# Four of six conditioning quads move from the recurrence to the next two norms' borders, where products use both PSUM bank rings

## The chip, the cores and the metric

One core of one Trainium2 chip runs the kernel. The metric is the device time of one execution in microseconds (us). The engines run their own streams of instructions and wait for one another by semaphores: TensorE (PE; its weight loads are listed as PEld), VectorE (DVE), ScalarE (ACT), GpSimd (POOL), and SyncE (SP), which here issues the DMAs.

## The reference, cut to what matters

One step of a trunk of two layers on 1024 prompt rows and 8 single decode rows. Layer 0 mixes by a gated linear recurrence with 8 heads (HGRN2), layer 1 by sliding-window attention over K and V that are projected once, after layer 0. Every sub-layer is scaled, shifted and gated by vectors of the condition c:

```
def rms_norm(x, g):
    x32 = x.astype(jnp.float32)
    y = x32 * lax.rsqrt(jnp.mean(x32 * x32, axis=-1, keepdims=True) + EPS)
    return y * g.astype(jnp.float32)

def modulate(x, g, shift, scale):
    return rms_norm(x, g) * (1.0 + scale[:, None, :]) + shift[:, None, :]

def ada_params(c, w, b):
    return (jax.nn.silu(c) @ w + b).astype(jnp.float32)

def swiglu(x, w_in, w_out):
    gate, up = jnp.split(x @ w_in, 2, axis=-1)
    return (jax.nn.silu(gate) * up) @ w_out

for l in range(DEPTH):                       # DEPTH = 2, D_MODEL = 1024
    sh1, sc1, g1, sh2, sc2, g2 = jnp.split(ada_params(c, w_ada[l], b_ada[l]), 6, axis=-1)
    xn = modulate(h, norm_w[l, 0], sh1, sc1)
    mix = hgrn2_mixer(xn, ...) if l < N_A_LAYERS else swa(xn @ w_q_b[j], k_sh, v_sh, ...) @ w_o_b[j]
    h = h + g1[:, None, :] * mix
    xn = modulate(h, norm_w[l, 1], sh2, sc2)
    h = h + g2[:, None, :] * swiglu(xn, w_ffn_in[l], w_ffn_out[l])
    if l == N_A_LAYERS - 1:
        sh_kv, sc_kv = jnp.split(ada_params(c, w_ada_kv, b_ada_kv), 2, axis=-1)
        k_sh, v_sh = jnp.split(modulate(h, kv_norm_w, sh_kv, sc_kv) @ w_kv, 2, axis=-1)
```

The conditioning is thus c (9 rows, the prompt's and the 8 samples') times 14 x 1024 columns of weights: 2 x 6 x 1024 of w_ada and 2 x 1024 of w_ada_kv.

## The kernel before, in words

All products keep about fp32 accuracy: a weight and a moving operand are each split into a high and a low part, and mm3 (L275 to L278) issues three matmuls for each tile of 128 rows. The 1032 columns (1024 prompt rows and 8 decode rows) go in three chunks of 344 (grouping G3) or in four of 258 (G4). A product's PSUM bank comes from one of two rings of four banks: mmp, tag "mm", and axp, tag "ax"; a product that takes its bank from mmp has four banks to run ahead in. The result is added to the residual stream h by VectorE (residual, L665, and L669 for the decode columns), which frees the bank.

**Conditioning.** The 14 x 1024 columns are seven "quads" of 2048 columns. A quad is eight steps (ada_step, L464), one for each 128 rows of the weight: two tiles of 128 x 1024 (512 KB each) are loaded (ada_unit, L269), and four fp32 matmuls with the 32-column stationary tile cT, one for each column group of TensorE, add 512 columns each into one bank. ada_end copies the bank, turns it by four transposes (L478) and adds the bias; mod_scale(m) makes the scale of norm m from it. Quad 0 is done at the start. Quads 1 to 6 are done in the recurrence: hgrn_proj(hh), heads 1 to 6, does two steps behind each of its four projections. Quad 6 is that of w_ada_kv. Norm 1 is the norm before the FFN of layer 0, 2 that before K/V, 3 that before q, 4 that before the FFN of layer 1. cT lies in a single buffer with the tag "early"; the tile "late" (the attention's biases) takes the same buffer later and is filled by 16 small DMAs in biases (L1075, L1076), which ffn(0) calls in its middle.

**Recurrence.** run interleaves two generators, hgrn_proj of a head (three chunks of four projections) and hgrn_core of the head before it, by a ratio.

**Border 1.** wo_first and wo_second multiply the two halves of the attention output with w_o. wo_second goes over four chunks of 258 and eight row tiles n, each one wo_product of 12 matmuls, then N.square for the norm's sums; finishing a chunk's norm and applying it is put on a list (later), and step() takes one piece of it at a time. Then ffn(0) begins with the gate and up products (proj). Beside them factors(x) makes sums and differences of x's four quarters for a product in seven parts in place of eight; diff and part (L1175 to L1183, L1193, L1194) are wide VectorE instructions, and L1234 adds a bank of a seven-part product. The same code makes border 3 in layer 1, from the sliding-window attention's output.

**Border 2.** The last pass of ffn(0) is again wo_product, three chunks of 344, with the norm before K/V (ToKV) beside it; then h is stored to hsc (L1404), four K/V products a chunk follow, and the norm before q is applied to X beside them. Weights are loaded by split_unit (L188) through three buffers named raw, cast on ScalarE (L175) and subtracted on GpSimd (L178).

The engines' streams are laid out when the program is built: each engine works its own list in order. SP's list has all the loads and stores of this kernel, so a DMA that waits holds those behind it.

## Time and profile before

| | us |
|---|---|
| median of 3 runs | 2582.14 (2582.01 to 2587.13) |
| the profiled execution | 2581.89 |
| its span | 2580.1 |

The profile's page gives the busy time of each engine and the chain of work that ended last. The costliest groups of instructions on TensorE and VectorE, by line, engine and operation, then the operands (out<-in), the shapes, the count, the busy time with the mean in ns of one, and the idle time ahead of them with what ended most of it:

```profile
L276 PE MATMUL mm<-c,wu 128*128 128x344 f32 (+1 forms) x2544 | 819.9, 323 | 21.4 <-DVE tdec L669 7.5
L276 PE MATMUL mm<-xq,wu 128*128 128x258 f32 x1448 | 412.1, 285 | 11.2 <-DVE c L1234 10.2
L665 DVE SCALAR_TENSOR_TENSOR c<-mm,ada,c 128x344 f32<-128x344 f32 (+3 forms) x400 | 220.6, 556 | 266.2 <-PE mm L278 265.2
```

A matmul of 344 columns starts every 0.16 us while its record is about 0.32 us long, because neighbours overlap; so the cost of a piece of TensorE work is read from start to start. The conditioning's loads are 96 tiles of w_ada and 16 of w_ada_kv:

```profile
c<-in_w_ada_dram SPq DMA_DIRECT2D x96, 512.0 KB
c<-in_w_ada_kv_dram SPq DMA_DIRECT2D x16, 512.0 KB
```

### The profile page before, as it was taken

The page shows a single profiled execution, that of the slowest core. Times are in us where ns is not written, and L with a number is a line of the kernel's source. Part 1 is how long each engine was busy: PE and PEld are TensorE (multiplying, and loading weights), DVE is VectorE, ACT ScalarE, POOL GpSimd, SP SyncE. Part 2 cuts the span into 40 slices and gives each one's busy share as a digit, 9 for nine tenths or more (in the row PEclk, how much of TensorE's full clock was granted, in tenths as well). Part 3 has the DMA queues.
Part 4 walks back from the last instruction along what each step waited for, and adds up shares of the span by engine and source line. Part 5 has one row for each costly group of instructions (what it writes and reads, how often), then busy time and mean ns, then how long its engine had stood idle before and what let it go on. Part 6 is the DMA issues. An engine that isn't in the chain of part 4 may idle for free.

```text
span 2580.1 us, 51430 instructions
## 1 busy us (share of the span) xinstructions
PE 2473.3 (96%) x21003; PEld 2337.4 (91%) x21003; DVE 1446.8 (56%) x3313; ACT 852.3 (33%) x1962; POOL 812.0 (31%) x604
## 2 busy tenths in 40 slices
PE   7999999999989999999999999999899999999998
PEld 5988888898989999999999897878899999999998
DVE  5343444446697554655433844576975555555336
ACT  4323222223343332333211445555433333332212
POOL 1211121212324443544432221203244444444321
PEclk9999999999999999999999999999999999999999
DMA  9464555514222224225421321432212222254201
GB/s 323 157 218 154 175 183 182 182 60 141 67 99 83 75 76 125 83 83 191 156 76 47 99 54 58 139 110 72 99 59 88 85 75 75 75 205 144 87 26 66
DMA packets 264670, 293.37 MB, mean 114 GB/s; under 512 B 28969, under 2 KB 223418, under 8 KB 264402
## 3 DMA queue, kind: packets, MB, share of 16 engines
q1 hardware_dynamic: 264032, 289.86, 34.1%
q8 instruction: 165, 2.70, 0.4%
q14 instruction: 71, 0.58, 0.1%
q10 hardware_dynamic: 402, 0.22, 0.0%
HBM read 231.27 MB, written 63.99 MB: 114 GB/s over the span
## 4 chain that ended last, share of the span: by engine, by line
PE 79%; DVE 12%; issue 4%; DMA 2%; ACT 1%; POOL 1%; SPq 1%; DVEq 0%; POOLq 0%; ACTq 0%
PE mm L276 18%; PE mm L278 18%; PE mm L277 18%; PE ax L276 5%; PE ax L277 5%; PE ax L278 5%; DVE w L646 2%; PE ax L1649 1%; PE ax L1578 1%; DMA c<-in_w_ada_dram 1%; PE ax L864 1%; PE ax L1635 1%; DVE xq L651 1%; DVE c L1182 1%; DVE c L1181 1%
## 5 line engine op out<-in xcount | busy, mean ns | idle before, releaser
L178 POOL TENSOR_TENSOR wu<-raw,wu 128x512 fp32r<-128x512 f32 x460 | 633.5, 1385 | 1397.4 <-ACT wu L175 1242.3
L276 PE MATMUL mm<-c,wu 128*128 128x344 f32 (+1 forms) x2544 | 819.9, 323 | 21.4 <-DVE tdec L669 7.5
L277 PE MATMUL mm<-c,wu 128*128 128x344 f32 (+1 forms) x2544 | 812.0, 319 | 8.0 <-DVE c L1313 6.5
L278 PE MATMUL mm<-c,wu 128*128 128x344 f32 (+1 forms) x2544 | 812.2, 319 | 0.3 <-issue 0.3
L276 PEld LDWEIGHTS mm<-c,wu 128*128 128x128 f32 x2544 | 482.3, 190 | 42.7 <-issue 22.3
L277 PEld LDWEIGHTS mm<-c,wu 128*128 128x128 f32 x2544 | 483.3, 190 | 12.8 <-DVE c L1313 7.6
L278 PEld LDWEIGHTS mm<-c,wu 128*128 128x128 f32 x2544 | 482.9, 190 | 4.9 <-issue 4.1
L175 ACT CAST wu<-raw 128x512 fp32r<-128x512 f32 x460 | 282.7, 620 | 593.7 <-PE mm L278 279.2
L276 PE MATMUL mm<-xq,wu 128*128 128x258 f32 x1448 | 412.1, 285 | 11.2 <-DVE c L1234 10.2
L278 PE MATMUL mm<-xq,wu 128*128 128x258 f32 x1448 | 411.4, 284 | 0.8 <-POOL wu L178 0.8
L277 PE MATMUL mm<-xq,wu 128*128 128x258 f32 x1448 | 411.5, 284 | 0.0
L665 DVE SCALAR_TENSOR_TENSOR c<-mm,ada,c 128x344 f32<-128x344 f32 (+3 forms) x400 | 220.6, 556 | 266.2 <-PE mm L278 265.2
L276 PE MATMUL ax<-xq,wu 128*128 128x258 f32 x1064 | 301.3, 283 | 0.0
L277 PE MATMUL ax<-xq,wu 128*128 128x258 f32 x1064 | 301.2, 283 | 0.0
L278 PE MATMUL ax<-xq,wu 128*128 128x258 f32 x1064 | 300.6, 283 | 0.0
L276 PEld LDWEIGHTS mm<-xq,wu 128*128 128x128 f32 x1448 | 275.1, 190 | 12.9 <-DVE c L1234 11.1
L278 PEld LDWEIGHTS mm<-xq,wu 128*128 128x128 f32 x1448 | 275.6, 190 | 1.2 <-POOL wu L178 1.1
L277 PEld LDWEIGHTS mm<-xq,wu 128*128 128x128 f32 x1448 | 275.9, 191 | 0.1
L277 PEld LDWEIGHTS ax<-xq,wu 128*128 128x128 f32 x1064 | 202.0, 190 | 0.0
L276 PEld LDWEIGHTS ax<-xq,wu 128*128 128x128 f32 x1064 | 201.6, 190 | 0.0
L278 PEld LDWEIGHTS ax<-xq,wu 128*128 128x128 f32 x1064 | 201.6, 189 | 0.0
L767 DVE TENSOR_TENSOR c<-c,mm 128x344 f32<-128x344 f32 x42 | 21.4, 513 | 126.6 <-ACT c L765 126.6
(301 smaller groups left out, 2831.2 us busy)
## 6 DMA issues: line engine op xcount, KB each, us to landing
c<-in_w_ada_dram SPq DMA_DIRECT2D x96, 512.0 KB
raw<-in_w_ffn_in_dram SPq DMA_DIRECT2D x152, 256.0 KB
ff<-c SPq DMA_DIRECT2D x44, 516.0 KB
c<-ff SPq DMA_DIRECT2D x44, 516.0 KB
raw<-in_w_ffn_out_dram SPq DMA_DIRECT2D x44, 512.0 KB
raw<-in_w_in_a_dram SPq DMA_DIRECT2D x32, 512.0 KB
out_dram<-c SPq DMA_DIRECT2D x16, 512.0 KB
c<-in_w_ada_kv_dram SPq DMA_DIRECT2D x16, 512.0 KB
```

The source lines that it names most:

```text
L175: i = act.copy(u[:, 0, :], src)
L178: eng.tensor_tensor(u[:, 1, :], src, u[:, 0, :], op=ALU.subtract)
L276: pe.matmul(ps, wh, xh, start=first, stop=False)
L277: pe.matmul(ps, wh, xl, start=False, stop=False)
L278: pe.matmul(ps, wl, xh, start=False, stop=last)
L646: dve.scalar_tensor_tensor(t, h[k][:, s], modA[:, m, k, 0:1], self.R[:, s], op0=ALU.mult, op1=ALU.mult)
L651: dve.scalar_tensor_tensor(xl, t, shift, xh, op0=ALU.add, op1=ALU.subtract)
L665: dve.scalar_tensor_tensor(hc, ps[:, : g.pl[c]], ada[:, gate + n, 0:1], hc, op0=ALU.mult, op1=ALU.add)
L864: pe.matmul(ps[32 * j : 32 * j + 32, c * 32 : (c + 1) * 32], KS[:, t0 : t0 + 32], QP[:, t0 : t0 + 32], start=True, stop=True, tile_positio ...
L1181: dve.tensor_tensor(t, flat(p[0]), flat(q[0]), op=ALU.subtract)
L1182: dve.tensor_tensor(e, flat(p[1]), flat(q[1]), op=ALU.subtract)
L1578: pe.matmul(psv[hf][:, gi, s0:256], q[2 * gp + gi][r, tb * P : (tb + 1) * P], kT[a][r, (tb - 1) * P + s0 : (tb + 1) * P], start=True, stop ...
```

## The change

The diff does six things. (1) anyp gives banks from the two rings in turn; wo_second and the last pass of ffn use it, in both layers. (2) The order in which conditioning tiles are loaded becomes quads 1, 2, 6, 3, 4, 5. (3) In the recurrence only heads 1 to 4 do conditioning, one step behind each projection: quad 1 in heads 1 and 2, quad 2 in heads 3 and 4. (4) A generator, conditioning, does the other quads a step at a time: 6 and 3 in wo_second of layer 0 (from the second chunk on, at five of eight row tiles), 4 and 5 in the last pass of ffn(0) (from the second chunk on, at each row tile); what is left is drained behind the loop. mod_scale(2), (3) and (4) are called there. (5) The x of K/V and the X of q are held in Triples, 18 tiles of three row tiles and one chunk each, in place of 16 tiles. (6) factors makes part 7 of both halves behind part 6 of both.

```diff
@@ -125,6 +125,13 @@
     def mmp():
         return pp.tile([P, 512], F32, tag="mm", name=nm("mm"), bufs=4)
 
+    turns = [0]
+
+    def anyp():
+
+        turns[0] += 1
+        return (mmp, axp)[turns[0] % 2]()
+
     def axp():
         return pp.tile([P, 512], F32, tag="ax", name=nm("ax"), bufs=4)
 
@@ -341,7 +348,7 @@
             for np_ in range(4):
                 wo_pair(w_ffn_out[l], j, np_)
 
-    for q in range(1, 7):
+    for q in (1, 2, 6, 3, 4, 5):
         ada_quad_units(q)
     for h in range(NH):
         for part in (1, 2, 0, 3):
@@ -569,6 +576,25 @@
                 xh, xl = (z[:, T:TOK] for z in self.t[k0 + k])
                 act.copy(xh, src[:, k, :])
                 dve.tensor_tensor(xl, src[:, k, :], xh, op=ALU.subtract)
+
+    class Triples:
+
+
+        def __init__(self, n):
+            self.q = [
+                [[p4.tile([P, 3, W], F32R, tag="c4", name=nm("xt")) for _ in range(2)] for _ in range(0, n, 3)]
+                for _ in range(NCH)
+            ]
+
+        def at(self, k, g, c):
+            return [z[:, k % 3, :] for z in self.q[c][k // 3]]
+
+        def decode(self, src):
+            for i, pair in enumerate(self.q[-1]):
+                ks = slice(3 * i, min(3 * i + 3, src.shape[1]))
+                xh, xl = (z[:, : ks.stop - ks.start, G3.pl[-1] :] for z in pair)
+                act.copy(xh, src[:, ks, :])
+                dve.tensor_tensor(xl, src[:, ks, :], xh, op=ALU.subtract)
 
     def quad():
         return tuple(p4.tile([P, 4, G4.w], F32R, tag="c4", name=nm("xq")) for _ in range(2))
@@ -749,7 +775,7 @@
     pool.memset(attT, 0.0)
 
     def hgrn_proj(hh):
-        cond = 1 <= hh <= 6
+        cond = 1 <= hh <= 4
         f = big()
         tiles = []
         for i in range(4):
@@ -772,12 +798,11 @@
             else:
                 tiles.append(t)
             if cond:
-                ada_step(hh, 2 * i)
-                ada_step(hh, 2 * i + 1)
+                ada_step((hh + 1) // 2, 4 * ((hh - 1) % 2) + i)
                 yield
         data[hh] = [f, kk] + tiles
-        if cond:
-            ada_end(hh)
+        if hh in (2, 4):
+            ada_end(hh // 2)
 
     def hgrn_first():
         us = ws.done[:4]
@@ -1083,14 +1108,23 @@
     for hh in range(NH):
         first = hgrn_proj(hh) if hh else hgrn_first()
         if hh:
-            run((first, 16 if hh < 7 else 12), (hgrn_core(hh - 1), 15))
+            run((first, 16 if hh <= 4 else 12), (hgrn_core(hh - 1), 15))
         else:
             run((first, 1))
             for k in range(KT):
                 sp.dma_start(xs[k], h[k])
 
-    for m in range(1, 5):
-        mod_scale(m)
+    mod_scale(1)
+
+    def conditioning(quads, mods):
+
+        for q in quads:
+            for k in range(KT):
+                ada_step(q, k)
+                yield
+            ada_end(q)
+        for m in mods:
+            mod_scale(m)
 
 
     def mixed(scr, i):
@@ -1110,8 +1144,8 @@
     def mixed_dec(o, dec, i):
         o.decode(dec[:, 4 * i : 4 * i + 4, :])
 
-    def wo_product(u, o, c, n, gate, tdec, g=G3):
-        ps = mmp()
+    def wo_product(u, o, c, n, gate, tdec, g=G3, bank=mmp):
+        ps = bank()
         for k in range(4):
             i = 2 * k + n % 2
             xh, xl = o.at(k, g, c)
@@ -1130,7 +1164,7 @@
                     yield
         residual_dec(tdec)
 
-    def wo_second(o, gate, m):
+    def wo_second(o, gate, m, beside=iter(())):
         tdec = small([P, KT, NB], "tdec", 2)
         us = [ws.next() for _ in range(4)]
         N = Norm(G4)
@@ -1143,14 +1177,18 @@
 
         for c in range(G4.n):
             for n in range(KT):
-                wo_product(us[n // 2], o, c, n, gate, tdec, G4)
+                wo_product(us[n // 2], o, c, n, gate, tdec, G4, anyp)
                 N.square(c, n)
                 if n >= 2:
                     step()
+                if c and n % 3:
+                    next(beside, None)
             if c == G4.last:
                 residual_dec(tdec)
                 N.square_dec()
             later.append(then(c))
+        for _ in beside:
+            pass
         return x
 
     def reload_h(src, *cs):
@@ -1195,7 +1233,8 @@
                 yield
                 xs7[i][6] = part(t1)
                 yield
-                t3 = diff(b22, b12)
+            for i in range(2):
+                t3 = diff(x[2 * i + 1][1], x[2 * i + 1][0])
                 yield
                 xs7[i][7] = part(t3)
                 yield
@@ -1207,7 +1246,7 @@
 
         return xs7, steps()
 
-    def ffn(l, x, norm, aside=None):
+    def ffn(l, x, norm, aside=None, beside=iter(())):
 
         gff = 48 * l + 40
         hs = dp.tile([KT, P, T], F32, name=f"hs{l}")
@@ -1351,10 +1390,12 @@
         us = [ws.next() for _ in range(4)]
         for c in range(NCH):
             for n in range(KT):
-                wo_product(us[n // 2], o, c, n, gff, tdec)
+                wo_product(us[n // 2], o, c, n, gff, tdec, bank=anyp)
                 last.square(c, n)
                 last.scale(c, n)
                 step()
+                if c:
+                    next(beside, None)
                 if c == LAST and n == 4:
                     last.early()
             if c == LAST:
@@ -1362,6 +1403,8 @@
                 last.square_dec()
                 last.scale_dec()
             later.append(last.then(c))
+        for _ in beside:
+            pass
         return last
 
 
@@ -1373,7 +1416,7 @@
     run((wo_first(o, 16), 12), (hgrn_tail, 28))
     o = mixed(osc, 1)
     mixed_dec(o, odec, 1)
-    X = wo_second(o, 16, 1)
+    X = wo_second(o, 16, 1, conditioning((6, 3), (2, 3)))
 
     class ToKV(Norm):
         def scale(self, c, k):
@@ -1387,7 +1430,7 @@
 
         def __init__(self):
             super().__init__()
-            self.x = Rows(KT)
+            self.x = Triples(KT)
 
         def then(self, c):
             self.finish(c)
@@ -1395,7 +1438,7 @@
             yield from self.apply_steps(c, 2, self.x)
 
     bs = []
-    nkv = ffn(0, X, ToKV, lambda: bs.extend(biases()))
+    nkv = ffn(0, X, ToKV, lambda: bs.extend(biases()), conditioning((4, 5), (4,)))
     late, biasd, gd, nsk, nskd = bs
 
 
@@ -1404,7 +1447,7 @@
         sp.dma_start(hsc[k], h[k])
     kvT = [big() for _ in range(4)]
     us = [ws.next() for _ in range(4)]
-    X = Rows(KT)
+    X = Triples(KT)
 
     for c in range(NCH):
         for n in range(4):
```

Line numbers of the changed kernel are 7 higher from L276 on, and some 25 to 43 higher further down: the conditioning's matmul is L471, its load L276, a weight's load L195, the loads of late L1100 and L1101, the store to hsc L1447, the wide subtractions of factors L1214 to L1232 and the add of a seven-part bank L1273.

**SyncE, at the end of ffn(0).** Rows of SP's list before; raw is a weight's buffer, c here a tile of h:

```order
L188 DMA raw_15820<-in_w_kv_dram 128x8x128
L1404 DMA hsc<-c_1583_13717 128x1024
L1404 DMA hsc<-c_1584_13719 128x1024
L188 DMA raw_16366<-in_w_kv_dram 128x8x128
L1404 DMA hsc<-c_1585_13721 128x1024
L1404 DMA hsc<-c_1586_13723 128x1024
L188 DMA raw_16374<-in_w_q_b_dram 128x8x64 x2
```

The same place in the changed kernel, in two pieces; the first shows the last two conditioning tiles, the second begins with the last two of the 16 loads of late:

```order
L276 DMA c_1951_16286<-in_w_ada_dram 128x1024
L276 DMA c_1952_16288<-in_w_ada_dram 128x1024
L1447 DMA hsc<-c_1550_13574 128x1024
L1447 DMA hsc<-c_1551_13576 128x1024
L1100 DMA late<-rd 16x127
L1101 DMA late<-rd 16x1
```
```order
L1100 DMA late<-rd 16x127
L1101 DMA late<-rd 16x1
L1447 DMA hsc<-c_1552_13578 128x1024
L1447 DMA hsc<-c_1553_13580 128x1024
L1447 DMA hsc<-c_1554_13582 128x1024
L1447 DMA hsc<-c_1555_13584 128x1024
L1447 DMA hsc<-c_1556_13586 128x1024
L195 DMA raw_16368<-in_w_kv_dram 128x8x128
L195 DMA raw_16376<-in_w_q_b_dram 128x8x64 x2
```

The 16 loads of late have moved from the middle of ffn(0) to a place behind the conditioning's last tiles; the first of them waits for the last conditioning matmul, since late takes cT's buffer. The fourth K/V weight (raw_16366 before, raw_16368 now) stood behind two stores and now stands behind two stores, the 16 loads and five more stores.

**TensorE, in the first chunk of K/V.** Rows of the changed kernel; xt is the norm's output, wu a weight, mm_16523 the bank of the third K/V product:

```order
L285 MATMUL mm_16481<-xt_15612,wu_15674 128x344
L283 MATMUL mm_16481<-xt_15614,wu_15674 128x344
L284 MATMUL mm_16481<-xt_15615,wu_15674 128x344
L285 MATMUL mm_16481<-xt_15614,wu_15674 128x344
L283 MATMUL mm_16481<-xt_15614,wu_15674 128x344
L471 MATMUL ax_16129<-c_1951_16286,cT 32x512 x2
L284 MATMUL mm_16481<-xt_15615,wu_15674 128x344
L285 MATMUL mm_16481<-xt_15614,wu_15674 128x344
L283 MATMUL mm_16523<-xt_15610,wu_15679 128x344
L284 MATMUL mm_16523<-xt_15611,wu_15679 128x344
L471 MATMUL ax_16129<-c_1952_16288,cT 32x512 x2
L285 MATMUL mm_16523<-xt_15610,wu_15679 128x344
```
```order
L285 MATMUL mm_16523<-xt_15614,wu_15682 128x344
L663 MATMUL ax_16470<-w_16468,ones 128x344
L1469 MATMUL ax_16867<-ident,c_1962_16366 128x128 x2
L283 MATMUL mm_16567<-xt_15610,wu_16370 128x344
L284 MATMUL mm_16567<-xt_15611,wu_16370 128x344
```

Before, no conditioning stood here. Now the last conditioning step (c_1951, c_1952) stands here as two visits of two matmuls with product matmuls between, and wu_16370, made from the fourth K/V weight, is used 22 product matmuls and eleven small ones (four transposes, four sums of one column, one of 344 columns, two transposes) later.

**VectorE, in factors.** Rows before, in layer 0; xq is a quarter or a part, and c_1081 collects the banks of a seven-part product:

```order
L1181 TENSOR_TENSOR c_1085_9056<-xq_7735,xq_7733 128x1032
L1182 TENSOR_TENSOR c_1086_9057<-xq_7736,xq_7734 128x1032
L1183 TENSOR_TENSOR c_1085_9056<-c_1085_9056,c_1086_9057 128x1032
L1176 TENSOR_TENSOR xq_9062<-c_1085_9056,xq_9061 128x1032
L1181 TENSOR_TENSOR c_1090_9091<-xq_7723,xq_8837 128x1032
L1182 TENSOR_TENSOR c_1091_9092<-xq_7724,xq_8838 128x1032
L1183 TENSOR_TENSOR c_1090_9091<-c_1090_9091,c_1091_9092 128x1032
L1176 TENSOR_TENSOR xq_9097<-c_1090_9091,xq_9096 128x1032
L1181 TENSOR_TENSOR c_1095_9126<-xq_7731,xq_9017 128x1032
L1182 TENSOR_TENSOR c_1096_9127<-xq_7732,xq_9018 128x1032
L1234 TENSOR_TENSOR c_1081_9023<-c_1081_9023,mm_9168 128x258
L1183 TENSOR_TENSOR c_1095_9126<-c_1095_9126,c_1096_9127 128x1032
```

And now, where c_1047 collects the banks:

```order
L1219 TENSOR_TENSOR c_1051_8911<-xq_7436,xq_7434 128x1032
L1220 TENSOR_TENSOR c_1052_8912<-xq_7437,xq_7435 128x1032
L1221 TENSOR_TENSOR c_1051_8911<-c_1051_8911,c_1052_8912 128x1032
L1214 TENSOR_TENSOR xq_8917<-c_1051_8911,xq_8916 128x1032
L1219 TENSOR_TENSOR c_1056_8946<-xq_7424,xq_8692 128x1032
L1273 TENSOR_TENSOR c_1047_8878<-c_1047_8878,mm_9023 128x258
L1220 TENSOR_TENSOR c_1057_8947<-xq_7425,xq_8693 128x1032
L252 TENSOR_TENSOR raw_9161<-raw_9161,raw_9164 128x512
L1221 TENSOR_TENSOR c_1056_8946<-c_1056_8946,c_1057_8947 128x1032
L1273 TENSOR_TENSOR c_1047_8878<-c_1047_8878,mm_9049 128x258
```

Before, ten wide subtractions stand ahead of the first add of c_1081; now five of them stand ahead of the first add of c_1047. 

## The prediction

> **What bounds the kernel now.** First the page: busy shares, then the chain that ended last.
>
> ```profile
> span 2580.1 us, 51430 instructions
> PE 2473.3 (96%) x21003; PEld 2337.4 (91%) x21003; DVE 1446.8 (56%) x3313; ACT 852.3 (33%) x1962; POOL 812.0 (31%) x604
> PE 79%; DVE 12%; issue 4%; DMA 2%; ACT 1%; POOL 1%; SPq 1%; DVEq 0%; POOLq 0%; ACTq 0%
> ```
>
> TensorE works 96% of the span, so only 107 us of it are idle, and a change that moves TensorE work can gain no more than the idle time it fills. The 12% of the chain on VectorE say where that time lies. The stretches that the change touches, by windows (us, then busy time and count of each engine, granted clock, DMA share, GB/s):
>
> ```profile
> core 0: us, PE busy (x) PEld busy (x) DVE busy (x) ACT busy (x) POOL busy (x), PEclk, DMA share, GB/s
> 466.00:540.00 74.00, 69.51 (x878) 61.13 (x877) 32.76 (x76) 20.04 (x56) 13.14 (x10) 1.00 0.44 144
> 540.00:605.00 65.00, 61.52 (x803) 58.56 (x801) 35.11 (x75) 24.41 (x70) 18.93 (x15) 1.00 0.34 99
> 700.00:750.00 50.00, 41.53 (x314) 40.08 (x315) 44.50 (x122) 24.25 (x54) 15.44 (x14) 0.93 0.36 127
> 800.00:815.00 15.00, 10.44 (x75) 10.23 (x74) 11.85 (x14) 4.31 (x7) 4.80 (x4) 0.89 0.14 40
> 1461.00:1468.00 7.00, 5.72 (x20) 5.75 (x21) 6.02 (x15) 2.56 (x5) 3.76 (x4) 0.51 0.52 209
> 1800.00:1850.00 50.00, 41.58 (x324) 40.08 (x323) 46.85 (x119) 25.42 (x57) 16.82 (x16) 0.97 0.37 127
> 1900.00:1920.00 20.00, 15.48 (x117) 15.28 (x116) 16.82 (x16) 6.13 (x11) 5.68 (x4) 0.91 0.10 27
> ```
>
> The first two rows are one head of the recurrence with a quad beside it and one without: TensorE is full in both. The others are the three borders that the change touches: border 1 (attention product of layer 0, norm, start of its FFN; 690 to 815), border 2 (last FFN pass of layer 0, norm, K/V; 1406 to 1535), border 3 (as border 1, in layer 1; 1800 to 1920). VectorE is busy 44.5 and 46.9 of 50 us at borders 1 and 3, and TensorE only 41.5. TensorE's waits in the three borders (total us, times, longest):
>
> ```profile
> PE mm L276 <- DVE c L1234: 5.1, 2, 4.6
> PE mm L276 <- DVE c L665: 3.3, 2, 2.4
> PE ax L637 <- DVE w L630: 2.9, 1, 2.9
> PE mm L276 <- DVE tdec L669: 1.3, 1, 1.3
> PE ax L622 <- DVE c L619: 1.0, 1, 1.0
> ```
> ```profile
> PE mm L276 <- DVE tdec L669: 4.3, 1, 4.3
> PE ax L637 <- DVE w L630: 1.5, 1, 1.5
> PE ax L1431 <- ACT c L1427: 1.4, 1, 1.4
> PE mm L276 <- ACT c L650: 1.1, 1, 1.1
> PE mm L277 <- DVE c L571: 0.8, 1, 0.8
> ```
> ```profile
> PE mm L276 <- DVE c L1234: 5.1, 2, 4.5
> ```
>
> Border 1 waits 13.6 us and loses 50 x 0.07 + 15 x 0.11 = 5.1 more to the clock: 18.7 in all. Border 2 waits 9.1 (a row of 0.6 is left out) and loses 7 x 0.49 = 3.4. That is all there is to fill, and the waits for L665 and L669 are for a free bank of the ring "mm".
>
> **What a visit costs.** A "visit" is a run of conditioning matmuls (L464) between other work. Its price shows on TensorE's timeline, start to start; each fp32 matmul is two records:
>
> ```profile
> 237.88 0.39 PE L1000 MATMUL ax<-c,c 128*128 128x128 f32 x2
> 238.20 1.92 PE L464 MATMUL ax<-c,cT 128*32 128x512 f32 x16
> 240.05 0.42 PE L276 MATMUL mm<-c,wu 128*128 128x344 f32 x1
> 240.32 0.32 PE L277 MATMUL mm<-c,wu 128*128 128x344 f32 x1
> ```
> ```profile
> 120.98 0.62 PE L464 MATMUL ax<-c,cT 128*32 128x512 f32 x2
> 121.44 0.60 PE L464 MATMUL ax<-c,cT 128*32 128x512 f32 x2
> 121.87 0.54 PE L864 MATMUL ax<-c,c 128*32 128x32 f32 x37
> ```
>
> Two steps (eight matmuls) take 240.05 - 238.20 = 1.85, four column groups at a time. Half a step (two matmuls, two of the four groups) takes 121.87 - 120.98 = 0.89: as long as a whole step, because the other two groups lie idle. Going in and coming out add about 0.1 each (240.32 - 240.05 is 0.27 where 344-wide matmuls follow at 0.16). So I take 2.05 for eight matmuls and 1.05 for four or for two.
>
> The Trainium skill, "TensorEngine Tiling (Array Packing)", section Tiling Modes, says that tiles work independently, but that changing the tiling mode drains the array, and this speaks against many short visits. The rows agree with a drain of about 0.2 us a visit, so 39 more visits make 8 us of it, which the 1.05 holds already; without a drain the sum would be 8 us lower.
>
> **Recurrence.** Before there are 30 visits in heads 1 to 6 (22 of eight matmuls, eight small ones): 22 x 2.05 + 8 x 1.05 = 53.5 us. In the changed order 18 small ones are left: 18.9. That removes 34.6. The two windows bear it out: a head with a quad is about 74 us, one without about 65, and two heads lose a quad, four lose half. TensorE idles 3 to 5 us in either kind, so I take all of it: **-34.6**.
>
> **Border 1.** 24 visits, nearly all of two matmuls, since each of the two 512 KB tiles of a step is used as it lands: +25.2. Against that stand 18.7 us of loss. The 4.6 for L665 and L669 and the clock loss of 3.5 go, since eight banks let TensorE run on and the visits stand in the gaps. The 5.1 before L1234 and its clock loss of 1.6 go by the new order in factors (next part). The 3.9 for L630 and L619 I leave: that chain of the norm's sums ends as late as before. So -14.8, and the border costs **+10.4**. If everything is filled it is 6.5; if VectorE, which stays as full as it was, still ends last in the 50 us window, about 15.
>
> **factors, both layers.** A difference and its part are three instructions (L1181 to L1183) and one more:
>
> ```profile
> L1181 DVE TENSOR_TENSOR c<-xq,xq 128x1032 f32<-128x1032 f32 x3 | 4.8, 1590 | 0.0
> L1176 DVE TENSOR_TENSOR xq<-c,xq 128x1032 fp32r<-128x1032 f32 x5 | 6.9, 1382 | 3.3 <-ACT xq L1175 3.3
> ```
>
> About 5 us, and in the changed order one such group less stands ahead of the add L1234 that frees the bank TensorE waits for. Border 3, where VectorE binds and a second ring cannot help, gains this alone: 4.5 of wait and 20 x 0.09 = 1.8 of clock, less about 1 since the group still has to be done: **-5**. Bounds: nothing (the wait moves to part 7) and -8.
>
> **Border 2.** 27 visits, one of eight, one of six, 25 of two: 2.05 + 1.5 + 25 x 1.05 = +29.8. Filled: the 4.3 for a bank, the 3.4 of clock, and the 1.5 for L630, since visits now lie between, 9.2 in all; the other 3.3 lie behind the visits and stay. That is +20.6.
>
> Then a **new wait**. The tile "late" shares its buffer with cT, which the conditioning now needs until its last step inside the K/V stage. Its 16 small loads, done at 977.9 to 993.7 before, now stand on SP behind the last weight tiles and wait for that step; behind them stand five stores to hsc and the fourth K/V weight. Prices (start, us, queue):
>
> ```profile
> 977.92 2.04 SPq L1075 DMA_DIRECT2D late<-rd x1
> ...
> 992.76 0.42 SPq L1075 DMA_DIRECT2D late<-rd x1
> 993.23 0.42 SPq L1076 DMA_DIRECT2D late<-rd x1
> 1445.91 0.38 SPq L188 DMA_DIRECT2D raw<-in_w_kv_dram x1
> ```
> ```profile
> L1404 SPq DMA_DIRECT2D hsc<-c x8: 319/329/339, 1442.2 to 1466.7; - x8
> ```
> ```profile
> GB/s 33 0 0 16 0 0 377 401 270 139 434 401 74 6 128 270 344 393 431 393 131 172 377 295 197 102 288 287 292 88 0 0 0 0 0 0 35 151 282 287
> ```
> ```profile
> L178 POOL TENSOR_TENSOR wu<-raw,wu 128x512 fp32r<-128x512 f32 x460 | 633.5, 1385 | 1397.4 <-ACT wu L175 1242.3
> L175 ACT CAST wu<-raw 128x512 fp32r<-128x512 f32 x460 | 282.7, 620 | 593.7 <-PE mm L278 279.2
> ```
>
> The third fence is the DMA rate from 1440 to 1460 in 40 slices; it peaks near 400 GB/s. From the last step: 16 issues at 993.23 - 992.76 = 0.47 are 7.5 us; five stores of 512 KB at 400 GB/s end 6.6 later, 14.1; the weight's 512 KB 1.3 and about 1 to land, 16.4; cast 0.62 and subtraction 1.39, 18.4. In that time TensorE has 22 product matmuls at 0.16 and eleven small ones, about 5.5 us (counted in its changed order, whose first and last rows stand with the change). So it stands about **13 us**. Before, this weight was issued at 1445.91, far ahead of its use, and nothing waited. The clock after it: window 1461 to 1468 shows 0.51 for 7 us behind a wait of 4.3, so about 3 us of work are lost. Border 2 in all: 20.6 + 13 + 3 = **+36.6**. Bounds for the stall: 7 (stores and issues overlap fully) to 21 (the loads at the 15.7 us that they took from 977.92 to 993.65).
>
> The Trainium skill, "TensorE: Matmul & The Clock Gate", Part 1, says that an idle window of about 3.4 us halves the clock and that one busy window of that length restores it. The trace has twice that, 7 us at 0.51. By the page the loss would be 1.7 and the sum 1.3 lower; the row decides.
>
> **Small parts.** The X of K/V and q takes 18 tiles where it took 16, so two slots fewer are free for weight tiles; mod_scale moves with its quads; a decode of three tiles replaces one of eight. All of it lies beside TensorE: 0, with 3 us at worst if a slot comes late.
>
> **Sum** against the profiled execution's 2581.89 (the median, 2582.14, is the same to 0.01%): -34.6 + 10.4 - 5 + 36.6 = +7.4, so 2589.3, say **2589**. TensorE's own work grows by 20 (55 us of short visits at the borders replace 34.6), and the new wait eats what the filling brings.
>
> **Rivals.** (a) *Not slower: the fourth weight is no wait.* Its price is the 16 us of wait and clock at border 2. If stores and small loads overlap, or TensorE has more left behind the last step, the stall shrinks; it decides from about 5 us of stall on. Without it the sum is -9, about 2573, and with every gap at borders 1 and 2 filled (3.9 + 3.3) 2566. For it: the stores are only 0.33 to issue. Against it: one queue, and the order on SP is fixed. Faster by over 0.2% (5.2 us, about what a measurement of this kernel can tell): 0.25. (b) *It cancels:* a stall of 7 to 8 and a loss of 1.5 by the clock give -34.6 + 10.4 - 5 + 29.6 = 0.4, 2582: 0.33. (c) *Weight tiles come late at the borders.* A border needs 16 MB in about 80 us beside its own weights. Tiles of 512 KB at 400 GB/s take 1.3 us where visits come every 2 or so, so the rate is enough, but a slot comes free only eight tiles ahead. If a third of the visits wait 1 us, +17: 2606. Chance 0.12. (d) *The second ring does nothing*, because VectorE ends last in any case: border 1 fills 6 less, 2595; it is in the forecast's case. That case, slower by 5 to 20 us, has 0.30.
>
> **How the numbers follow.** Slower is (c) and the forecast, 0.42; same 0.33; faster 0.25. The forecast's own range is 2583 to 2600. The range for 8 in 10 goes from rival (a) without its last fillings, 2570, to (c), 2606.
>
> **What would show it.** Recurrence: the heads 5 and 6 near 65 us, 1 to 4 near 70. Border 1: no wait for L665's successor, and visits of about 1 us start to start. Border 3: the wait for the add at L1234 gone. Border 2: TensorE waiting some 13 us for the weight from w_kv, with "late" issuing right before it on SP, and a granted clock near 0.5 behind it. The prediction is wrong if that wait is under 5 us, if visits of two matmuls cost under 0.8 us, or if waits for in_w_ada_dram appear.

## The result, and the profile after

| | before | changed |
|---|---|---|
| median, us | 2583.27 (2582.01 to 2587.13, 4 runs) | 2604.24 (2600.23 to 2609.42, 4 runs) |
| ratio, 95% interval | | 1.008 (1.0056 to 1.0103) |
| profiled execution, us | 2581.89 | 2609.42 |

The changed kernel is slower by 0.8%, 21 us by the medians. Its profiled execution is the longest of its four, 27.5 us above that of before, so the stages below add up to more than the medians' difference. The page of the changed kernel, busy shares and the chain's shares by engine:

```profile
span 2607.6 us, 51392 instructions
PE 2514.4 (96%) x21003; PEld 2347.4 (90%) x21003; DVE 1438.0 (55%) x3303; ACT 849.4 (33%) x1952; POOL 808.6 (31%) x604
PE 84%; DVE 6%; issue 4%; DMA 3%; POOL 1%; ACT 1%; SPq 1%; DVEq 0%; POOLq 0%; ACTq 0%
```

VectorE's share of the chain fell from 12% to 6%: gaps were filled. But TensorE's idle time, span less busy time, fell only from 106.8 to 93.2 us, while its busy time rose by 41 us (slow clock counts as busy) with the same count of instructions, 21003. The work that filled the gaps takes more time than they held.

Both kernels issue 15216 product matmuls of mm3 in the same sequence of stages, so the time at which the nth starts, counted from the first (at 37.6 us before), in one trace and the other, says where the difference arises. What each stage adds against the profile before, in us (the headings give the end of each stage in the profile before; all the runs are listed, since the experiments are read by it):

| kernel | recurrence, to 672 | border 1, to 840 | ffn(0), to 1400 | border 2, to 1548 | attention, to 1793 | border 3, to 1936 | rest |
|---|---|---|---|---|---|---|---|
| changed | -26.9 | 13.1 | 0.0 | 35.6 | 3.2 | 5.1 | -2.8 |
| e1_late | -26.4 | 12.9 | -0.5 | 31.3 | -0.5 | 2.9 | -3.0 |
| e2_whole | -29.2 | 4.9 | -1.0 | 23.8 | 0.3 | 3.0 | -3.8 |
| e3_ring | -30.5 | 12.9 | -1.0 | 36.2 | 0.3 | -1.1 | -2.4 |
| e4_factors | 4.8 | -1.9 | 0.4 | -0.2 | -0.6 | -0.8 | -1.6 |
| e5_unmoved | 4.3 | 3.4 | 1.5 | -3.0 | 2.2 | 5.4 | -1.3 |
| e6_all | -26.4 | 5.0 | -1.0 | 16.9 | -0.5 | -0.9 | -1.3 |
| e7_unmoved_ring | 1.8 | -1.9 | 0.7 | -3.2 | 6.3 | -1.0 | -2.0 |
| e8_three | -14.5 | 5.2 | -2.7 | 3.5 | 0.2 | 0.6 | -1.6 |
| e9_onering | -28.0 | 3.3 | -0.6 | 16.9 | -0.3 | -1.1 | -2.2 |
| e10_minimal | -26.6 | 3.3 | -2.6 | 27.4 | 2.7 | 1.2 | -1.7 |
| e11_triples | -30.0 | 3.3 | -1.3 | 17.2 | 0.1 | 0.0 | -2.5 |

The recurrence is the same in before, e4, e5 and e7, and yet it differs by up to 4.8 us; attention and the rest, in which the kernels differ little (tile layouts, the ring of the last FFN pass), scatter by 6.9 and 2.5 us from kernel to kernel. Much of this is the clock: e4's recurrence has two windows of 3.4 us at 0.50 (at 334.5 and 484.7) and e7's one at 0.51 (at 482.2), and each costs 1.7 us; the changed kernel's attention has one of 7 us at 0.53 (1714 to 1721, where before has 1.00), which is its 3.2. So a difference of 2 us in one row of one stage says nothing, and one of 5 in the recurrence or in attention little.

**Border 1** has next to no idle time left. TensorE's waits in the changed kernel from 678 to 802 (total us, times, longest), and its windows (columns as in the prediction):

```profile
PE mm L283 <- DVE c L1273: 1.2, 1, 1.2
```
```profile
678.00:730.00 52.00, 51.86 (x355) 35.09 (x355) 37.72 (x99) 21.29 (x47) 15.05 (x14) 1.00 0.69 234
730.00:780.00 50.00, 50.00 (x418) 49.94 (x417) 39.82 (x68) 15.77 (x32) 14.36 (x8) 1.00 0.31 115
```

Of the 13.6 us of waits 1.2 are left, and the slow clock is gone, and still the border is 13 us longer: 24 visits cost more than the gaps held.

**Border 2** shows the new wait. SyncE's queue, TensorE's two longest waits and the windows of the changed kernel:

```profile
1483.47 0.32 SPq L1100 DMA_DIRECT2D late<-rd x1
...
1490.33 0.42 SPq L1101 DMA_DIRECT2D late<-rd x1
1490.79 4.19 SPq L1447 DMA_DIRECT2D hsc<-c x5
1495.07 1.15 SPq L195 DMA_DIRECT2D raw<-in_w_kv_dram x1
```
```profile
PE mm L283 <- ACT wu L182: 7.7, 1, 7.7
PE ax L1469 <- ACT c L1456: 4.5, 1, 4.5
```
```profile
1492.00:1506.00 14.00, 4.17 (x13) 3.33 (x14) 9.72 (x27) 5.01 (x12) 2.51 (x2) 0.52 0.98 292
```

The last visit ends at 1483.4; the 16 loads begin at once, behind them five stores, and the weight is issued 11.6 us after the first load. TensorE stands 12.6 us and then runs at about half clock to 1506. There is a second wait that I had not looked for, 4.5 us for ScalarE's copy c (L1456). The copy that ends this wait starts at 1493.25. ScalarE's list has the copy of the last quad's bank (L482) and the norm's work ahead of it, VectorE's list the bias add of that quad (L488), and both engines stood over 12 us until the last conditioning step was done. Rows of ScalarE's timeline and one of VectorE's (start, length, idle ahead of it and its releaser):

```profile
1483.48 0.58 ACT L482 COPY c<-ax 128x512 f32<-128x512 f32 x1 [12.63 <-PE ax L471]
...
1493.25 0.42 ACT L1456 COPY c<-mm 128x344 f32<-128x344 f32 x1
```
```profile
1484.89 0.50 DVE L488 TENSOR_TENSOR ada<-ax,bT 128x36 f32<-128x36 f32 x4 [12.72 <-PE ax L485]
```

**Border 3** has no conditioning, and its waits were not filled but moved. Before, besides the 5.1 for L1234, and then in the changed kernel, with two of its windows:

```profile
PE mm L276 <- DVE c L665: 3.4, 2, 2.4
PE ax L637 <- DVE w L630: 2.9, 1, 2.9
PE mm L276 <- DVE tdec L669: 1.9, 1, 1.9
```
```profile
PE mm L283 <- DVE c L1273: 5.0, 3, 3.5
PE ax L648 <- DVE c L645: 4.7, 2, 4.5
PE mm L283 <- ACT c L1267: 2.3, 1, 2.3
```
```profile
1854.00:1861.00 7.00, 5.90 (x29) 5.90 (x30) 4.78 (x24) 0.83 (x2) 0.63 (x1) 0.52 1.01 348
1875.00:1885.00 10.00, 9.27 (x41) 8.83 (x42) 4.87 (x22) 1.89 (x6) 0.00 (x0) 0.50 0.13 52
```

The waits for a free bank (L665, L669) are gone; in their place TensorE waits 4.5 us in one piece for the norm's sums (L645), later 2.3, and behind either the clock is at half, for 7 and for 10 us. The waits add up to 12 us where they were 13.3; it is the clock that makes the border longer. From 1825 to 1950 the granted clock is 0.93, 0.90 and 0.93 in stretches of 50, 50 and 25 us, a loss of 10 us, where the two windows in the prediction lose 1.5 + 1.8.

### The profile page after: what moved, and what is told of

Its sections match the earlier page's. It is cut to its first block, busy times and chain, and to the rows that moved or that the text cites. A ratio compares the mean times of both kernels' runs of the same rounds, so it can differ in the third digit from the quotient of the medians.

```text
span 2607.6 us, 51392 instructions
## 1 busy us (share of the span) xinstructions
PE 2514.4 (96%) x21003; PEld 2347.4 (90%) x21003; DVE 1438.0 (55%) x3303; ACT 849.4 (33%) x1952; POOL 808.6 (31%) x604
## 4 chain that ended last, share of the span: by engine, by line
PE 84%; DVE 6%; issue 4%; DMA 3%; POOL 1%; ACT 1%; SPq 1%; DVEq 0%; POOLq 0%; ACTq 0%
PE mm L283 19%; PE mm L285 18%; PE mm L284 18%; PE ax L283 6%; PE ax L284 6%; PE ax L285 6%; PE ax L471 2%; PE ax L1621 1%; PE ax L1692 1%; PE ax L1678 1%; PE ax L889 1%; DMA c<-in_w_ada_dram 1%; POOL wu L185 1%; DVE w L672 1%; PE ax L1001 1%
## 5 line engine op out<-in xcount | busy, mean ns | idle before, releaser
L283 PE MATMUL mm<-c,wu 128*128 128x344 f32 (+1 forms) x2032 | 660.3, 326 | 5.8 <-ACT c L676 4.1
L284 PE MATMUL mm<-c,wu 128*128 128x344 f32 (+1 forms) x2032 | 653.4, 322 | 6.8 <-DVE c L1352 6.4
L285 PE MATMUL mm<-c,wu 128*128 128x344 f32 (+1 forms) x2032 | 652.9, 321 | 0.0
L283 PEld LDWEIGHTS mm<-c,wu 128*128 128x128 f32 x2032 | 385.7, 190 | 30.1 <-issue 15.6
L284 PEld LDWEIGHTS mm<-c,wu 128*128 128x128 f32 x2032 | 386.7, 190 | 14.1 <-DVE c L1352 7.6
L285 PEld LDWEIGHTS mm<-c,wu 128*128 128x128 f32 x2032 | 386.5, 190 | 5.4 <-issue 4.7
L691 DVE SCALAR_TENSOR_TENSOR c<-mm,ada,c 128x344 f32<-128x344 f32 (+3 forms) x344 | 192.8, 563 | 268.7 <-PE mm L285 268.0
L283 PEld LDWEIGHTS mm<-xq,wu 128*128 128x128 f32 x1448 | 277.0, 191 | 12.5 <-DVE c L1273 8.1
L283 PE MATMUL mm<-xt,wu 128*128 128x344 f32 x288 | 94.2, 328 | 7.7 <-ACT wu L182 7.7
```

Of the source, the lines that this page charges most:

```text
L283: pe.matmul(ps, wh, xh, start=first, stop=False)
L284: pe.matmul(ps, wh, xl, start=False, stop=False)
L285: pe.matmul(ps, wl, xh, start=False, stop=last)
L691: dve.scalar_tensor_tensor(hc, ps[:, : g.pl[c]], ada[:, gate + n, 0:1], hc, op0=ALU.mult, op1=ALU.add)
```

## The experiments

Ratios are to the kernel before, timed on the same chip beside each group of kernels.

**e1_late: the small loads elsewhere.**

```diff
@@ biases()
-            sp.dma_start(biasd[16 * b : 16 * b + 16, 1:P], rd[:, P : 2 * P - 1])
-            sp.dma_start(biasd[16 * b : 16 * b + 16, 0:1], rd[:, 2 * P - 1 : 2 * P])
@@ behind the K/V loop
     kT, vT = kvT[:2], kvT[2:]
+    fill()      # the 16 loads
```

> The changed kernel, but the 16 small loads of the tile late are traced behind the K/V stage, so that on SyncE the fourth K/V weight no longer stands behind them. Theory (the SP queue behind the last conditioning step makes the stop at border 2): the waits for the weight's cast (7.7 us) and subtraction (0.4 us) go and most of the slow clock behind them, the 4.5 us for L1456 stay; 9 to 12 us below the changed kernel, about 2593. Rival (ScalarE and VectorE, which stood 12.6 us behind the copy and the bias add of the last quad, hold TensorE anyway): TensorE still stands 10 us or more in the first K/V chunk and the time is within 3 us of the changed kernel, 2601 to 2607.

Measured: 2599.31 us, 1.0052 (1.0036 to 1.0068). TensorE's waits in the first K/V chunk:

```profile
PE ax L1474 <- ACT c L1460: 4.5, 1, 4.5
PE mm L283 <- ACT wu L182: 3.3, 1, 3.3
```

The wait for the weight falls from 7.7 to 3.3 and border 2 from 35.6 to 31.3. So the queue on SyncE was part of the stop. What stays does not come from the queue: the weight is now issued even before the last visit, and ScalarE casts it 22 us later:

```profile
1474.63 0.38 SPq L195 DMA_DIRECT2D raw<-in_w_kv_dram x1
1496.57 1.12 ACT L182 CAST wu<-raw 128x512 fp32r<-128x512 f32 x2
```

The cast stands in ScalarE's list behind the last quad's copy, for which ScalarE stood 12.63 us here too, and behind the norm's work. So 7.8 of the 12.6 us stay with the queue cleared, all of it behind ScalarE's list. The theory had one of two causes and claimed too much (9 to 12 us; measured 5 by the medians, 7 by the ratios); the rival named the other cause, but not to the end, since some time did come off.

**e2_whole: a step as one visit.** group(j) is the matmul on column group j; issue_after keeps groups 0 and 1 directly behind group 3.

```diff
-        for j in range(4):
-            pe.matmul(ada_ps[q][32 * j : 32 * j + 32, :], ...)
+        group(2)
+        i = group(3)
+        with tc.issue_after(i.ins):
+            group(0)
+            group(1)
```

> The changed kernel, but the two matmuls on the later tile of a conditioning step go first and the other two directly behind them, so that at the borders a step is one visit of four matmuls instead of two visits of two: 51 visits instead of 69. Theory (a visit has a fixed price of about 1.15 us whether it has two matmuls or four): 18 visits less take 16 to 21 us off, about 2585; a visit of four keeps about 1.0 us from start to start. Rival (the borders are long because VectorE or the tiles' DMA is late, so saved TensorE time turns into waits): less than 6 us come off, 2598 or more, and waits for L691, L695 or in_w_ada_dram appear.

Measured: 2583.07 us, 0.9985 (0.9973 to 0.9998); against the changed kernel that is 21 us by the medians and 25 by the ratios, at or a little above the theory's 16 to 21. Two visits of half a step in the changed kernel, then one of a whole step here, on TensorE's timelines:

```profile
1460.40 1.05 PE L471 MATMUL ax<-c,cT 128*32 128x512 f32 x4
1461.38 0.42 PE L285 MATMUL ax<-c,wu 128*128 128x344 f32 x1
...
1462.21 1.05 PE L471 MATMUL ax<-c,cT 128*32 128x512 f32 x4
1463.19 0.42 PE L283 MATMUL ax<-c,wu 128*128 128x344 f32 x1
1463.45 0.32 PE L284 MATMUL ax<-c,wu 128*128 128x344 f32 x1
```
```profile
1441.54 0.31 PE L285 MATMUL ax<-c,wu 128*128 128x344 f32 x1
1441.78 1.07 PE L472 MATMUL ax<-c,cT 128*32 128x512 f32 x8
1442.78 0.43 PE L283 MATMUL mm<-c,wu 128*128 128x344 f32 x1
```

Four records take 1461.38 - 1460.40 = 0.98, eight take 1.00. With what it costs to go in (0.24 where matmuls follow at 0.16) and out (0.26), a visit is about 1.17 us, full or half full. Border 1 falls by 8.2 and border 2 by 11.8, though TensorE now reaches the late weight sooner and waits 9.7 us for it. Counted in the traces, border 1 has 24 visits and then 17, border 2 27 and then 15; at 1.17 us that is 8.2 and 14.0, less the 2.0 by which the wait grew.

**e3_ring: layer 1's wo_second on one ring.**

```diff
-                wo_product(us[n // 2], o, c, n, gate, tdec, G4, anyp)
+                wo_product(us[n // 2], o, c, n, gate, tdec, G4, bank)    # anyp in layer 0, mmp in layer 1
```

> The changed kernel, but wo_second of layer 1 takes its banks from the ring mm alone, as before the change; layer 0 and the FFN's last passes keep both rings. Theory (at border 3, where no conditioning fills the gaps, running ahead on eight banks only puts the wait off to a place where it is longer and the clock falls): border 3 becomes 5 us shorter than before the change instead of 5 longer, so 8 to 11 us off, about 2595. Rival (the later part 7 in factors lengthens border 3): no change, 2601 to 2607, and the waits for L1273 stay at 5 us.

Measured: 2598.56 us, 1.0048 (1.0032 to 1.0064). Border 3 goes from +5.1 to -1.1: the second ring made it longer. But it does not become 5 us shorter than before the change. Two of its waits at border 3:

```profile
PE mm L283 <- DVE c L1273: 4.2, 1, 4.2
PE mm L283 <- DVE c L691: 3.4, 2, 2.4
```

The wait for the add of a seven-part bank, which the new order in factors was to remove, is there again, 4.2 us. The next run takes this up.

**e4_factors: the order in factors alone, in the kernel before.**

```diff
-                t3 = diff(b22, b12)
+            for i in range(2):
+                t3 = diff(x[2 * i + 1][1], x[2 * i + 1][0])
```

> The kernel before with one edit, the new order in factors (part 7 of both halves behind part 6 of both). Theory (the wide VectorE work ahead of the first add of a seven-part product was the wait of 4.5 us at borders 1 and 3): both waits go with their slow clock, 4 to 6 us at each border, so 8 to 12 us below the kernel before, about 2573. Rival (the wait moves to part 7's first use or to the next add): within 3 us of the kernel before.

Measured: 2584.31 us, 0.9996 (0.9986 to 1.0006): the rival's. The wait at border 1, and that at border 3:

```profile
PE mm L276 <- DVE c L1235: 4.3, 1, 4.3
```
```profile
PE mm L276 <- DVE c L1235: 4.2, 1, 4.2
```

4.6 and 4.5 us have become 4.3 and 4.2. In VectorE's timeline the add that ends the wait at border 1 (L1234 at 808.19 before, L1235 at 811.33 here) has the same eleven wide instructions of lines L1176 to L1183 between it and the add before it in both kernels. The new order doesn't shorten the row that TensorE waits behind.

**e5_unmoved and e7_unmoved_ring: the rings without moved conditioning.** Both keep the conditioning in the recurrence as before; e5 has both rings wherever the change has them, e7 in the FFN's last passes alone.

```diff
-    for q in (1, 2, 6, 3, 4, 5):
+    for q in range(1, 7):
-        cond = 1 <= hh <= 4
+        cond = 1 <= hh <= 6
-                ada_step((hh + 1) // 2, 4 * ((hh - 1) % 2) + i)
+                ada_step(hh, 2 * i)
+                ada_step(hh, 2 * i + 1)
...
-    X = wo_second(o, 16, 1, conditioning((6, 3), (2, 3)))
+    X = wo_second(o, 16, 1)
-    nkv = ffn(0, X, ToKV, lambda: bs.extend(biases()), conditioning((4, 5), (4,)))
+    nkv = ffn(0, X, ToKV, lambda: bs.extend(biases()))
```

> The changed kernel with the conditioning left in the recurrence as before the change (six quads, two steps to a visit), and the rest of the change kept: both rings in wo_second and in the FFN's last passes, Triples, the order in factors. Theory (without visits to fill the gaps both rings help at border 2 alone, where the bank was the only wait, and cost 5 us at each of borders 1 and 3, where VectorE ends last): border 2 6 to 8 us shorter, borders 1 and 3 5 longer each, in all 0 to 4 above the kernel before. Rival (the rings by themselves fill the gaps and the moved conditioning only spoils it): all three borders shorter, 8 us or more below the kernel before.

> As e5_unmoved, but wo_second of both layers on the ring mm, so that both rings serve the FFN's last passes alone. Theory: border 2 keeps its 6 to 8 us, borders 1 and 3 stand as before the change, so 6 to 8 us below the kernel before. Rival (the bank wait at border 2 moves to the norm's chain of ScalarE and VectorE instructions): within 3 us of the kernel before, and the waits for L1456's or L571's counterparts grow by as much.

Measured: e5 2593.57 us, 1.0021 (1.0009 to 1.0033); e7 2581.74 us, 0.9986 (0.9976 to 0.9996). The waits of TensorE in e5 that add up to most, at border 1 and at border 2:

```profile
PE ax L648 <- DVE c L645: 5.7, 3, 4.5
```
```profile
PE ax L648 <- DVE c L645: 8.5, 2, 6.7
```

At borders 1 and 3 both rings cost 3.4 and 5.4 us (with one ring, -1.9 and -1.0). At border 2 the bank wait of 4.3 us is gone, and 6.7 for the norm's sums stand there (in e7 too); border 2 gains 3 us, not 6 to 8. So e5 lies above its theory's 0 to 4 us (5 by the ratio), with its costs where the theory had them, and e7 gains 4 to 5 us, between its theory and its rival, whose wait it shows. By itself the second ring gains little, and that at border 2 alone: it lets TensorE do early what it will then wait behind.

**e6_all: the three repairs together** (e1, e2 and e3 in one kernel).

> The changed kernel with three edits together: the small loads of late behind the K/V stage, a conditioning step as one visit, and wo_second of layer 1 on the ring mm. Theory (three separate prices of the change, which add up): whole visits 21 us, the wait for the fourth K/V weight 6 to 9 of the 14 us that TensorE stood in the first K/V chunk with whole visits, border 3 5 us; about 2570, 0.6% below the kernel before; the 4.5 us for L1456 stay. Rival (the prices overlap, since the time saved at border 2 is waited for there by ScalarE's copies): not below 2578.

Measured: 2575.36 us, 0.996 (0.9946 to 0.9975). Faster than the kernel before by 0.4%, though not by 0.6: between theory and rival. By the medians the three repairs bring 5, 21 and 6 us one by one and 29 together, so they add up but for 3 us (by the ratios 40 and 31, but for 9); the 4.5 us for the copy and 3.3 for the weight stay, as in e1.

**e8_three: three quads stay in the recurrence,** border 2 does one.

```diff
-    for q in (1, 2, 6, 3, 4, 5):
+    for q in (1, 2, 5, 6, 3, 4):
-        cond = 1 <= hh <= 4
+        cond = 1 <= hh <= 6
-    nkv = ffn(0, X, ToKV, lambda: bs.extend(biases()), conditioning((4, 5), (4,)))
+    nkv = ffn(0, X, ToKV, lambda: bs.extend(biases()), conditioning((4,), (4,)))
```

> As e6_all, but three quads stay in the recurrence (1, 2 and 5, half a quad a head in heads 1 to 6), border 1 keeps 6 and 3, and border 2 does quad 4 alone, which ends inside the FFN's last pass. Theory (what holds TensorE at border 2 is that the conditioning reaches into the K/V stage: ScalarE and VectorE wait in order for the last quad, and the fourth K/V weight for SyncE's queue): the stops of 4.5 and 3.3 us and the slow clock go, about 8 to 10 us, while the eight steps cost the same 9 us in either place; about 2567, 0.7% below the kernel before. Rival (the last chunk's norm chain holds TensorE there in any case, as the 6.7 us for L645 in e7_unmoved_ring): a wait of 4 us or more for the norm's chain takes their place and the time stays within 4 us of e6_all, 2572 to 2579.

Measured: 2573.98 us, 0.9962 (0.9949 to 0.9975), the same as e6_all. TensorE's one wait over 0.3 us at border 2:

```profile
PE ax L655 <- DVE c L652: 5.3, 1, 5.3
```

Border 2 falls from 16.9 to 3.5, and the recurrence gives 12 back. The waits for the copy and the weight are gone, and 5.3 us for the norm's chain stand in their place: the rival's. With no conditioning left in the K/V stage, TensorE waits for the K/V stage's own norm.

**e9_onering: the repairs, with all products on one ring.**

```diff
-                wo_product(us[n // 2], o, c, n, gate, tdec, G4, bank)
+                wo_product(us[n // 2], o, c, n, gate, tdec, G4)
-                wo_product(us[n // 2], o, c, n, gff, tdec, bank=anyp)
+                wo_product(us[n // 2], o, c, n, gff, tdec)
```

> As e6_all, but all products on the ring mm, as before the change. Theory (with visits in the stream TensorE comes to each bank later, so the visits alone fill the gaps and the second ring adds little): border 1 and border 2 within 3 us of e6_all each, 2575 to 2580. Rival (the second ring is what lets the visits fill the gaps): the waits for L691's and L695's counterparts come back at borders 1 and 2, 4 us or more each, 2583 or more.

Measured: 2571.66 us, 0.9952 (0.9936 to 0.9968). All of TensorE's waits from 660 to 800, border 1:

```profile
PE ax L670 <- DVE w L663: 1.4, 1, 1.4
PE mm L283 <- ACT c L1333: 0.8, 1, 0.8
PE mm L283 <- DVE c L1284: 0.4, 1, 0.4
PE ax L472 <- DMA c<-in_w_ada_dram: 0.2, 1, 0.2
```

No wait for a bank, with four banks as before. The visits alone put the products far enough apart; the second ring adds nothing beside them either. Nor does it at border 2, 16.9 as in e6_all.

**e10_minimal and e11_triples: what else is needed.** e10 is e9 with the old order in factors and x of K/V and q as whole-width tiles; e11 is e10 with Triples.

```diff
-            self.x = Triples(KT)
+            self.x = Rows(KT)
...
-    X = Triples(KT)
+    X = Rows(KT)
```

> As e9_onering, but factors in its old order and the x of K/V and q in 16 tiles as before the change, so that of the change the moved conditioning alone is left, with whole-step visits and the loads of late behind the K/V stage. Theory (banks, order in factors and Triples each bring nothing measurable, the moved conditioning in whole steps brings all of it): within 4 us of e9_onering, ratio 0.994 to 0.997. Rival (the moved conditioning needs the two free slots less or the earlier add that Triples and factors change): 5 us or more slower than e9_onering, ratio 0.998 or more.

> As e10_minimal, but with the x of K/V and q in Triples as in the change; the old order in factors stays. Theory (the 13 us between e9_onering and e10_minimal are Triples': its tiles are taken a chunk at a time, so the slots stay free for conditioning tiles until they are needed, and border 2 was 10 us longer without): ratio 0.994 to 0.997, border 2 about 17 us longer than before the change where e10_minimal has 27, no wait of 4 us for a bank and none of 5 us for in_w_ada_dram there. Rival (the order in factors makes the difference): ratio 0.998 or more, and border 2 as in e10_minimal.

Measured: e10 2584.71 us, 0.9995 (0.9985 to 1.0005), where I had expected no difference from e9; e11 2571.71 us, 0.9958 (0.9942 to 0.9975). Waits of e10 at border 2:

```profile
PE ax L472 <- DMA c<-in_w_ada_dram: 5.7, 4, 2.5
PE mm L283 <- DVE tdec L702: 4.3, 1, 4.3
```

So factors' order brings nothing, and Triples, which I had put down at 0, are worth 10 us at border 2 (27.4 against 17.2). Sixteen whole-width tiles take their slots at the first chunk; six of Triples' eighteen do. With Rows the conditioning's tiles come late, as SyncE's rows of e10 and then of e11 show:

```profile
1442.38 26.95 SPq L276 DMA_DIRECT2D c<-in_w_ada_dram x20
```
```profile
1403.97 40.04 SPq L276 DMA_DIRECT2D c<-in_w_ada_dram x21
```

In e10 no visit starts between 1421.5 and 1451.0, the last five steps stand in one piece at 1467.4, and the gaps they should fill stay open; in e11 a visit comes every 2 to 6 us from 1402.9 to 1454.3.

## Why the prediction was right in direction, and what it had wrong

The forecast was slower with 2589, and the kernel is slower, but by 21 us where 7 were said. 2604.24 lies outside the forecast's own range, 2583 to 2600, and inside the whole range only because that went to 2606 for rival (c), which did not occur: that part is luck. The profiled execution stands 20.1 us above the sum, and the stages account for it: recurrence 7.7, border 1 2.7, border 2 -1.0, border 3 10.1, attention 3.2, the rest -2.8. By the prediction's own steps:

- **Recurrence, -34.6: right mechanism, mis-sized.** Measured -26.9 against the profile before, and about -30 against the mean of the four kernels with an unchanged recurrence (0, 4.8, 4.3, 1.8). Heads 5 and 6 take 65.5 us each, as said, and heads 1 to 4 68.4 to 71.6. TensorE's windows over heads 1 to 4 and heads 5 and 6 (a head's four projections are 288 product matmuls), before and then changed:

```profile
93.10:386.80 293.70, 279.06 (x3495) 1.00 0.56 184
386.80:534.10 147.30, 139.12 (x1759) 1.00 0.50 164
```
```profile
93.20:374.80 281.60, 267.40 (x3361) 0.99 0.40 132
374.80:505.90 131.10, 124.76 (x1626) 1.00 0.23 70
```

  A whole quad is worth 16.2 / 2 = 8.1 us a head, where 4 x 2.05 = 8.2 was taken. Losing half a quad gives back 12.1 / 4 = 3.0 us a head where 4.1 or more was counted. Part of the shortfall is the clock: two windows of 3.4 us in heads 2 and 3 of the changed kernel (at 181.8 and 253.5) are at 0.50, which is 3.4 us of work lost. Head 1 was the other error: before, it took 72.4 us, 6.8 more than head 7 without a quad, where its ten visits had been counted as 12.5. Why its eight small visits are cheap was not tested; the rows show them between other matmuls on 32 columns (L864).
- **Border 1, +10.4: right,** 13.1. The filling came as said, and more of it (17.5 of the 18.7 us, not 14.8); the visits cost 24 x 1.17 = 28, not 25.2, and 2.6 us are left without an account. In the trace 14 of the 24 visits have two matmuls, not nearly all; since a whole step takes as long, the sum is not touched. The 5.1 + 1.6 counted there for factors was the wrong reason: e10, with the old order, stands at +3.3 just as e9. The waits for L1234's add go when the visits come, not by the order.
- **factors and border 3, -5: the step that failed,** twice. The order gains 0.3 us of wait (e4_factors), since the work ahead of the add is the same. And I said that where VectorE binds a second ring "cannot help" and took that for no cost; it cost 5 to 6 us (e3_ring, e5_unmoved): TensorE runs ahead, waits 4.5 us in one piece instead of 1.0, 2.4 and 1.9 apart, and the clock is at half for 7 and 10 us.
- **Border 2, +36.6: right in size,** 35.6, with the wait at its place, in its order and at its length: the 13 us were 12.6. The weight's cast began 18 us after the last visit, where 16.4 were worked out; of these, the "about 1 to land" stands in no row, and the weight took 6.4 us from its issue at 1495.07 to its cast, behind five stores. But the cause was only part of it. The 16 loads and ScalarE's list run side by side, and each holds TensorE: with the loads cleared away 7.8 of the 12.6 us stay (e1_late), and with the copy in time TensorE would still have met the weight at 1502.
- **Rivals.** (a), not slower, fell: the stores did not overlap with the small loads (the five stores are issued from 1490.79 on, behind the last of them). (c), late weight tiles, did not occur in the changed kernel; e10 shows it for the layout that the change left behind. (d), that the second ring does nothing, held more than was granted: it gains nothing beside the visits (e9_onering) and costs at border 3.
- **The clock.** Window 1492 to 1506 has 0.52, but TensorE stands in most of it: about 4 us of matmuls run at half clock behind the stop. That is near the 3.4 us of one window that the Trainium skill, "TensorE: Matmul & The Clock Gate", Part 1, gives, while border 3 shows 7 and 10 us at half. Both occur, and the trace decides.
- **The drain.** The Trainium skill, "TensorEngine Tiling (Array Packing)", section Tiling Modes, says that a change of tiling mode drains the array, and gives no price. The trace agrees with about 0.2 us a visit for going in and out (0.08 + 0.10), which for e2_whole's 18 or 19 visits less is some 3 of its 21 us; the rest is that half a step takes as long as a whole one, 0.98 and 1.00. That the 0.2 us is the drain is not shown by a run of its own.
- **Small parts, 0: wrong for Triples,** which are worth 10 us at border 2.

What stays open: how much of the changed kernel's 27.5 us in its profiled execution against 21 by the medians is chance. Attention's 3.2 are a stretch at half clock, which e1, e2 and e3 don't have there; but in the recurrence these three have two to four stretches of 3.4 us, as the changed kernel has.

## What to carry to other kernels

Filling gaps of an engine is worth the gap minus the price of the visit, and short visits have a fixed price: make each a whole unit (here all four column groups) before moving it. A deeper ring of buffers helps only if the consumer catches up; where it ended last anyway, here at border 3, running ahead turned several short waits into a long one. When a step moves, follow every buffer that it keeps alive and every in-order list that waits for its end; here the loads behind one shared buffer, and the work behind one copy, stopped TensorE for 12.6 us.

## What was not expected of the hardware

- A visit on two of four column groups takes as long as on all four: 0.98 and 1.00 us.
- A stop of about 2 us can be enough to halve the clock, and for longer than it lasts: behind 2.3 us at 1875 the clock was 0.50 for 10 us, and behind 2.0 us at 180.6 in the changed kernel for 3.4. The length varies: behind 4.5 us at 1855 it was 7 us.
- Programs that differ only elsewhere differ by up to 4.8 us in an unchanged recurrence, mostly by such stretches (two of 3.4 us in e4_factors, one in e7_unmoved_ring), so a single profile's stage is not good to better than some us.
